# FFN down projection as 2x2 blocks with seven products, residual sum in DRAM

## The chip, the cores and the metric

The kernel runs on one core of one Trainium2 chip. The time is the device time of one launch in microseconds (us); the time before is the median of three runs. The profile is of one execution of the same program.

## What is computed

One layer of a hybrid encoder on 576 frames (512 of a new stream, 64 of a running one, the same weights for both): state-space heads and attention heads side by side, then an FFN, then a final norm. The change concerns the FFN alone; `x` there is what the two mixers and `w_out` have left.

```python
D_MODEL = 1024
D_FF = 2816          # 22 tiles of 128

def rmsnorm(x, w):
    return x * lax.rsqrt(jnp.mean(x * x, axis=-1, keepdims=True) + EPS) * w

x = x + jnp.concatenate([y_ssd, o], axis=-1) @ p['w_out']
hf = rmsnorm(x, p['norm_ffn'])
x = x + (jax.nn.silu(hf @ p['w_gate']) * (hf @ p['w_up'])) @ p['w_down']
y = rmsnorm(x, norm_final)
```

All in float32.

## The kernel before

**Layout.** Features lie on the 128 partitions and the T = 576 frames of both streams along the free axis, mostly in two halves of TH = 288 columns (`HC`). The residual `x2` is eight tiles of 128 x 576 in SBUF, one for each 128 of the 1024 features.

**Products.** A product of two float32 tiles is three matmuls: each operand is split into a high part (ScalarE's cast to fp32r, `wh_...`, L112) and a remainder (VectorE's subtraction, `wl_...`, L113), and high x high, high x low and low x high are summed in PSUM. `weights` (L119) loads 128 x 1024 raw weights on SyncE's queue and splits them.

**Gate and up.** For each of the FT = 22 FFN tiles f, `gu_steps` computes g (gate) and u (up) for both halves of the columns as one 2x2 block product with seven products in place of eight, m1 to m7, each with four contraction tiles (L852, 84 matmuls a tile). `gu_weights` makes the sums of weight blocks on VectorE (L809 to L812), `combine` and the steps m1 to m7 put the seven results together (copies of ScalarE at L914, L918, L922, additions of VectorE at L926 to L939; L935 and L939 are two of them). Three PSUM banks (tags sc, pp, hm) hold the results of a tile. The last two products of a tile, m4 and m3, are issued after m1 of the next one (`late`). `finish` takes silu of g (ScalarE), multiplies u by it (VectorE, L899) and splits the result into a high part and a remainder (`split_scaled`, L142 and L144): `prod[f]`, the operand of the down projection.

**Down.** CUTS divides the 22 tiles into five parts, of 5, 5, 4, 4 and 4. When the first tile of the next part has been computed, `down(fs)` runs the part just done: for each of the 8 output tiles t a weight tile of 128 x 128 for each f in it (`weights`, 512 or 640 columns, wr_d, wh_d, wl_d), and for each half of the columns `down_half` with 3 matmuls for each f (L953, ps_d), whose sum VectorE adds onto x2 (L966; in the first part x2 is first scaled by Ri, L965). The last part (f from LAST = 18 on) goes with the final norm: L953 ps_l with the weights wr_dl and the addition of `add` (L1005), then the outputs.

**Buffers.** tpool holds 7 tiles of one row of 576 (g, u and other temporaries), wpool 7 raw weight tiles, w2pool 11 split ones, cpool 5 pairs of rows (prod). midp's tags bc and sz hold x2. A tile that takes a buffer waits until the last reader of the one before is done.

**Order.** The steps are written as Python calls, but the order in which each engine issues its instructions is a list of numbers, ISSUE, one entry per engine, which is written into the program by hand or by a planner. Before, GpSimd has no instruction in the FFN's stage until the end.

## Time and profile before

| | before |
|---|---|
| median of 3 runs | 655.55 us (654.63 to 655.71) |
| span of the profiled execution | 651.7 us |
| median above the span | 3.9 us (655.55 - 651.7) |
| PE (TensorE) busy | 639.9 us, 98%, 4731 matmuls |
| DVE (VectorE) busy | 512.4 us, 79% |
| ACT (ScalarE) busy | 339.3 us, 52% |
| POOL (GpSimd) busy | 41.3 us, 6% |
| DMA | 63.22 MB, 97 GB/s over the span |

Busy times are sums over the span and say nothing of a single stage; the rows of the 40 slices, of stretches and of groups of instructions do. PE rows come one every 0.13 us where matmuls of 288 columns follow each other, though each row shows a duration of about 0.3 us, since they are pipelined. In the rows a name such as ps_d or wl_gu_S is the tile's name in the program without its numbers; "x165" is a count.

### The profile page before, as it was taken

The page shows a single profiled execution, that of the slowest core. Times are in us where ns is not written, and L with a number is a line of the kernel's source. Part 1 is how long each engine was busy: PE and PEld are TensorE (multiplying, and loading weights), DVE is VectorE, ACT ScalarE, POOL GpSimd, SP SyncE. Part 2 cuts the span into 40 slices and gives each one's busy share as a digit, 9 for nine tenths or more (in the row PEclk, how much of TensorE's full clock was granted, in tenths as well). Part 3 has the DMA queues.
Part 4 walks back from the last instruction along what each step waited for, and adds up shares of the span by engine and source line. Part 5 has one row for each costly group of instructions (what it writes and reads, how often), then busy time and mean ns, then how long its engine had stood idle before and what let it go on. Part 6 is the DMA issues. An engine that isn't in the chain of part 4 may idle for free.

```text
span 651.7 us, 11921 instructions
## 1 busy us (share of the span) xinstructions
PE 639.9 (98%) x4731; PEld 611.8 (94%) x4731; DVE 512.4 (79%) x935; ACT 339.3 (52%) x630; POOL 41.3 (6%) x80
## 2 busy tenths in 40 slices
PE   9999999998999999999999999999999999999995
PEld 8898989885787899999999999999999999999995
DVE  6899987899776699999996776775768577876655
ACT  7645426769674567665523445223533345334364
POOL 1321104001010000000000000000000000000023
PEclk9999999999999999999999999999999999999998
DMA  8312375323220232133422233311232224222004
GB/s 314 127 62 70 93 171 143 113 66 129 86 76 33 99 102 92 65 109 103 131 80 97 79 101 101 110 66 65 81 114 98 98 66 128 68 98 98 2 1 145
DMA packets 26151, 63.22 MB, mean 97 GB/s; under 512 B 3418, under 2 KB 10088, under 8 KB 25840
## 3 DMA queue, kind: packets, MB, share of 16 engines
q1 hardware_dynamic: 24560, 60.77, 28.3%
q0 software_dynamic: 816, 1.13, 0.8%
q8 instruction: 37, 0.61, 0.4%
q10 hardware_dynamic: 720, 0.57, 0.3%
q14 instruction: 18, 0.15, 0.1%
HBM read 58.03 MB, written 3.30 MB: 94 GB/s over the span
## 4 chain that ended last, share of the span: by engine, by line
PE 84%; DVE 3%; ACT 1%; DMA 1%; issue 1%; POOL 0%; POOLq 0%; DVEq 0%; ACTq 0%
PE ps_x L852 21%; PE ps_d L953 18%; PE ps_z L852 10%; PE ps_o L443 8%; PE ps_y L852 5%; PE ps_in L128 4%; PE ps_z L443 3%; PE ps_l L953 3%; PE ps_p L852 2%; PE sc L657 2%; PE pv L704 1%; PE ptp L679 1%; PE ps_v L590 1%; PE ps_q L443 1%; PE ps_y L527 1%
## 5 line engine op out<-in xcount | busy, mean ns | idle before, releaser
L953 PE MATMUL ps_d<-pr,wh_d 128*128 128x288 f32 x576 | 115.4, 294 | 0.0
L852 PE MATMUL ps_x<-xop,wh_gu_S 128*128 128x288 f32 x504 | 101.8, 295 | 0.0
L953 PEld LDWEIGHTS ps_d<-pr,wh_d 128*128 128x128 f32 x576 | 92.5, 188 | 0.0
L953 PE MATMUL ps_d<-pr,wl_d 128*128 128x288 f32 x288 | 84.6, 295 | 0.0
L852 PEld LDWEIGHTS ps_x<-xop,wh_gu_S 128*128 128x128 f32 x504 | 80.6, 188 | 0.2
L113 DVE TENSOR_TENSOR wl_gu_S<-gu,wh_gu_S 128x1024 fp32r<-128x1024 f32 x44 | 53.6, 1224 | 34.4 <-PE ps_y L852 13.8
L852 PE MATMUL ps_x<-xop,wl_gu_S 128*128 128x288 f32 x252 | 73.4, 295 | 0.0
L112 ACT CAST wh_gu_S<-gu 128x1024 fp32r<-128x1024 f32 x44 | 46.3, 1052 | 48.4 <-PE ps_d L953 25.4
L953 PEld LDWEIGHTS ps_d<-pr,wl_d 128*128 128x128 f32 x288 | 54.0, 188 | 0.0
L852 PEld LDWEIGHTS ps_x<-xop,wl_gu_S 128*128 128x128 f32 x252 | 47.0, 188 | 0.0
L128 PE MATMUL ps_in<-xs,wh_in 128*128 128x288 f32 x256 | 45.2, 298 | 1.2 <-DVE sp_a L351 1.0
L112 ACT CAST wh_d<-wr_d 128x640 fp32r<-128x640 f32 (+1 forms) x32 | 21.5, 673 | 39.1 <-PE ps_x L852 14.8
L128 PEld LDWEIGHTS ps_in<-xs,wh_in 128*128 128x128 f32 x256 | 37.5, 188 | 2.3 <-ACT up L381 1.2
L852 PE MATMUL ps_z<-xop,gu_a 128*128 128x288 f32 x252 | 38.0, 296 | 0.0
L852 PE MATMUL ps_z<-xop,wh_gu_S 128*128 128x288 f32 x168 | 36.0, 296 | 0.0
L852 PE MATMUL ps_x<-xop,wh_gu_A 128*128 128x288 f32 x168 | 35.3, 298 | 0.0
L852 PEld LDWEIGHTS ps_z<-xop,gu_a 128*128 128x128 f32 x252 | 35.1, 188 | 0.0
L852 PE MATMUL ps_y<-xop,wh_gu_A 128*128 128x288 f32 x168 | 34.2, 294 | 0.0
L966 DVE TENSOR_TENSOR x<-ps_d,x 128x288 f32<-128x288 f32 x64 | 28.8, 453 | 6.7 <-PE ps_d L953 6.5
L112 ACT CAST wh_gu_A<-gu 128x1024 fp32r<-128x1024 f32 x22 | 23.1, 1049 | 17.5 <-PE ps_d L953 11.5
L113 DVE TENSOR_TENSOR wl_gu_A<-gu,wh_gu_A 128x1024 fp32r<-128x1024 f32 x22 | 26.9, 1223 | 5.2 <-PE ps_x L852 3.9
L1049 POOL TENSOR_TENSOR fz<-fz,sq 128x320 f32<-128x320 f32 x3 | 2.6, 880 | 445.3 <-ACT sq L1044 445.3
(339 smaller groups left out, 1643.7 us busy)
## 6 DMA issues: line engine op xcount, KB each, us to landing
gu<-in_w_gu SPq DMA_DIRECT2D x44, 512.0 KB, 3.7
wr_d<-in_w_down SPq DMA_DIRECT2D x16, 320.0 KB, 2.9
wr_in<-in_w_in SPq DMA_DIRECT2D x8, 512.0 KB, 4.0
wr_out<-in_w_out SPq DMA_DIRECT2D x8, 512.0 KB, 3.2
wr_d<-in_w_down SPq DMA_DIRECT2D x16, 256.0 KB, 2.7
cumb<-cumD SPq DMA_DIRECT2D x5, 512.0 KB, 4.6
x<-in_xT SPq DMA_DIRECT2D x2, 1152.0 KB, 7.5
wr_z<-in_w_in SPq DMA_DIRECT2D x4, 512.0 KB, 4.4
```

The costliest lines, as they stand in the source:

```text
L112: act.copy(hi, raw)
L113: dve.tensor_tensor(lo, raw, hi.bitcast(F32), ALU.subtract)
L128: pe.matmul(ps[:m, hf, :n], w, x[:, hf * n : (hf + 1) * n], start=start and k == 0 and i == 0, stop=stop and k == last and i == 2,)
L443: pe.matmul(ps[:, :n], w, x[:, cols], start=k == 0 and i == 0, stop=k == len(terms) - 1 and i == 2,)
L527: pe.matmul(py[64 * j : 64 * j + 64, p * P : p * P + L], xdt[:L, h * HD : (h + 1) * HD], wts[:L, h, :L], start=True, stop=True,)
L590: pe.matmul(ps[:n], l, r, start=j == 0, stop=j == 2)
L657: pe.matmul(s[:, :nk], qs[:, j, q0 : q0 + P], ks[:, j, :nk], start=True, stop=True)
L679: pe.transpose(pp[:, k : k + P], prs[p, i][:, j, b * P : b * P + P], ident)
L704: pe.matmul(pv[64 * j : 64 * j + 64, b * P :], V[b][:, h * HD : (h + 1) * HD], pts[p, b, j], start=b == 0, stop=True, skip_group_check=b > 0,)
L852: pe.matmul(ps, p, q, start=not onto and first and kp == kps[0] and j == 0, stop=onto or (last and kp == kps[-1] and j == 2), skip_group_c ...
L953: pe.matmul(ps, w, x[:, cols], start=first and k == 0 and i == 0, stop=last and k == len(terms) - 1 and i == 2,)
L966: dve.tensor_tensor(x2[t][:, cols], ps, x2[t][:, cols], ALU.add)
```

## The change

The down projection of the 16 tiles f = 2 to 17 becomes 2x2 block products with seven products in place of eight. The tiles are taken as pairs (f even, f odd): the two feature tiles are the block rows of an operand, the two halves of the columns its block columns.

- `finish` hands a tile of PAIRED to `finish_pair`, which writes the product of u and g into the pair's tile (L915). After the second tile of a pair, `pair_operands` makes the combined operands (differences at L927 to L929: T1 to T4) and splits them into high parts (ScalarE, L936: 1152, 576 and 288 columns) and remainders (VectorE, L937). Two tiles with tags bc and sz, where x2 lay, hold part of them.
- `down_plain` takes the first part (f = 0 and 1) as before, but ScalarE copies its results out of PSUM and GpSimd writes them to `acc[1]` in DRAM; x2, scaled by Ri, is written to `acc[0]`.
- `down_steps(fs, m)` does a pair of output tiles (2m + 1 and 2m) for a part of four tiles: it loads the eight weight blocks in one transfer (wr_d), makes their eight sums on VectorE (ws_d, L1030 to L1034), splits both (L1038, L1039), and runs products m1, m6, m7, m2, m5, m4, m3 of six matmuls each in the manner of the gate/up steps (L1050). Products 6, 5 and 3 are added onto product 1 in one bank and 4 onto 7. ScalarE copies the seven intermediate results out of PSUM (L1061), and four transfers of GpSimd with addition (`send`, L1064) bring them into acc in DRAM: dd (288 columns), db, dc and da (576 columns each).
- Two of the four steps of a part stand after the first tile of the next part, two after the second.
- After the last step the residual comes back into two tiles `sum`: a plain load of acc[0] for four tiles each on SyncE's queue (L1143) and additions of acc[1] by GpSimd, two tiles each (L1145).
- CUTS is (0, 2, 6, 10, 14, 18, 22), and the order of every engine from the FFN's stage on is a new one.

The core of the diff (empty lines left out):

```diff
     def finish(f, g, u):
         act.activation(g, g, AF.Silu)
+        if f in PAIRED:
+            finish_pair(f, g, u)
+            return
         dve.tensor_tensor(u, u, g, ALU.mult)
         s = slot(cpool, "c", f"pr{f}")
         split_scaled(s, u, None)
         prod[f] = hilo(s)
+    raw_pair, pair_ops, pair_tiles, pending = {}, {}, [], []
+    def finish_pair(f, g, u):
+        k, second = f // 2, f % 2
+        if not second:
+            raw_pair[k] = slot(cpool, "c", f"up{k}")
+        b = raw_pair[k]
+        dve.tensor_tensor(b[:, second], u, g, ALU.mult)
+        if second:
+            pending.append(lambda: pair_operands(k))
+    def pair_operands(k):
+        b = raw_pair[k]
+        if len(pair_tiles) < 2:
+            pair_tiles.append(midp.tile([P, 4, T], F32, tag=("bc", "sz")[len(pair_tiles)], name=f"pair{k}"))
+        z = pair_tiles[(k - 1) % 2].rearrange("p a b -> p (a b)").bitcast(F32R)
+        b = b.rearrange("p a (h n) -> p (a h) n", h=2)
+        d13, d4 = tmp(f"d13_{k}").rearrange("p (a n) -> p a n", a=2), tmp(f"d4_{k}", TH).unsqueeze(1)
+        dve.tensor_tensor(d13, b[:, 0:2], b[:, 1:4:2], ALU.subtract)
+        dve.tensor_tensor(b[:, 1], d13[:, 1], b[:, 0], ALU.subtract)
+        dve.tensor_tensor(d4[:, 0], b[:, 1], b[:, 2], ALU.add)
+        bh, bl = (slot(cpool, "c", f"{n}{k}").bitcast(F32R).rearrange("p a (h n) -> p (a h) n", h=2) for n in ("uph", "upl"))
+        th, tl = (z[:, 3 * TH * i : 3 * TH * i + 3 * TH].rearrange("p (a n) -> p a n", a=3) for i in range(2))
+        ops = {}
+        for raw, hi, lo, names in (
+            (b, bh, bl, ("B11", "T2", "B21", "B22")), (d13, th[:, 0:2], tl[:, 0:2], ("T1", "T3")), (d4, th[:, 2:], tl[:, 2:], ("T4",)),
+        ):
+            act.copy(hi, raw)
+            dve.tensor_tensor(lo, raw, hi.bitcast(F32), ALU.subtract)
+            for i, n in enumerate(names):
+                ops[n] = hi[:, i], lo[:, i]
+        pair_ops[k] = ops
...
-    def down_terms(fs, t):
-        w = weights(a["w_down"][t][:, fs[0] * P : (fs[-1] + 1) * P], len(fs) * P, f"d{fs[0]}_{t}")
-        return [(wk(w, k), prod[f]) for k, f in enumerate(fs)]
+    acc = [dpool.tile([KT, P, T], F32, name=f"acc{i}") for i in range(2)]
...
-    def down(fs):
-        for t in range(KT):
-            terms = down_terms(fs, t)
+    def down_plain(fs, ts):
+        n = 1024 // (len(fs) * P)
+        for t in ts:
+            if t % n == 0:
+                raw = wslot(wpool, f"wr_d{t}")
+                sp.dma_start(
+                    raw.rearrange("p (t c) -> p t c", t=n),
+                    a["w_down"][t : t + n][:, :, fs[0] * P : (fs[-1] + 1) * P].rearrange("t p c -> p t c"),
+                )
+                w = split_weights(raw, f"d{t}")
+            terms = [(wk(w, t % n * len(fs) + k), prod[f]) for k, f in enumerate(fs)]
+            dn = tmp(f"dn{t}")
             for hf, cols in enumerate(HC):
-                ps = fbank(("hm", "sc", "pp")[(2 * t + hf) % 3], f"ps_d{fs[0]}_{t}")
+                ps = fbank(("hm", "sc", "pp")[(2 * t + hf) % 3], f"ps_d{t}")
                 down_half(ps, terms, cols)
-                if fs[0] == 0:
-                    dve.tensor_tensor(x2[t][:, cols], x2[t][:, cols], Ri[:, cols], ALU.mult)
-                dve.tensor_tensor(x2[t][:, cols], ps, x2[t][:, cols], ALU.add)
-    CUTS = (0, 5, 10, 14, LAST, FT)
+                act.copy(dn[:, cols], ps)
+            pool.dma_start(acc[1][t], dn)
+            dve.tensor_tensor(x2[t], x2[t], Ri, ALU.mult)
+            pool.dma_start(acc[0][t], x2[t])
+    DOWN = {
+        1: (0, 4, "B11"), 2: (0, 5, "B21"), 3: (1, 6, "B22"), 4: (0, 1, "T4"), 5: (1, 0, "T1"), 6: (1, 4, "T2"), 7: (1, 2, "T3"),
+    }
+    def down_steps(fs, m):
+        ks = [f // 2 for f in fs[::2]]
+        blocks = lambda z: z.rearrange("p (c n) -> p c n", n=P)
+        raw, sums = wslot(wpool, f"wr_d{fs[0]}_{m}"), wslot(wpool, f"ws_d{fs[0]}_{m}")
+        r, q = blocks(raw), blocks(sums)
+        sp.dma_start(
+            raw.rearrange("p (t c) -> p t c", t=2),
+            a["w_down"][2 * m : 2 * m + 2][:, :, fs[0] * P : (fs[-1] + 1) * P].rearrange("t p c -> p t c"),
+        )
+        four = lambda z: z.rearrange("p (a b) n -> p a b n", a=2)
+        dve.tensor_tensor(
+            four(q[:, 0:4]), r[:, 0:4:2].unsqueeze(1).to_broadcast([P, 2, 2, P]), four(r[:, 1:7])[:, :, 0:3:2], ALU.add,
+        )
+        dve.tensor_tensor(q[:, 4:6], q[:, 0:2], r[:, 4:8:2], ALU.add)
+        dve.tensor_tensor(q[:, 6:8], q[:, 4:6], r[:, 5:8:2], ALU.add)
+        w = []
+        for z, b0 in ((r, 1), (q, 0)):
+            hi, lo = (blocks(wslot(w2pool, f"d{fs[0]}_{m}_{len(w)}{i}", F32R)) for i in "hl")
+            act.copy(hi[:, b0:], z[:, b0:])
+            dve.tensor_tensor(lo[:, b0:], z[:, b0:], hi.bitcast(F32)[:, b0:], ALU.subtract)
+            w.append((hi, lo))
+        x, y, z = (fbank(tag, f"ps_d{fs[0]}_{m}") for tag in ("sc", "pp", "hm"))
+        def product_of(i, ps, onto=False):
+            src, b0, name = DOWN[i]
+            hi, lo = w[src]
+            for n, k in enumerate(ks):
+                b = b0 + (n if src else 2 * n)
+                xhi, xlo = pair_ops[k][name]
+                for j, (p, v) in enumerate(((hi[:, b], xhi), (hi[:, b], xlo), (lo[:, b], xhi))):
+                    pe.matmul(
+                        ps, p, v, start=not onto and n == 0 and j == 0, stop=onto or (n == len(ks) - 1 and j == 2),
+                        skip_group_check=onto,
+                    )
+        db, dd = (stage[i][m % 2] for i in range(2))
+        da, dc = (tmp(f"{z}{fs[0]}_{m}") for z in ("da", "dc"))
+        L, R = HC
+        t0, t1 = 2 * m + 1, 2 * m
+        def put(out, ps, sign=1.0):
+            (act.copy(out, ps) if sign > 0 else act.mul(out, ps, sign))
+        def send(i, out, src):
+            pool.dma_start(out, src, accum_op=ALU.add)
+        def m1():
+            product_of(1, x)
+            put(dd, x)
+            send(0, acc[0][t0][:, L], dd)
+        def m6():
+            product_of(6, x, True)
+            put(db[:, L], x, -1.0)
+        def m7():
+            product_of(7, z)
+            put(dc[:, R], z)
+        def m2():
+            product_of(2, y)
+            put(da[:, L], y)
+        def m5():
+            product_of(5, x, True)
+            put(db[:, R], x, -1.0)
+            send(0, acc[0][t1], db)
+        def m4():
+            product_of(4, z, True)
+            put(dc[:, L], z)
+            send(1, acc[1][t1], dc)
+        def m3():
+            product_of(3, x, True)
+            put(da[:, R], x)
+            send(1, acc[1][t0], da)
+        return m1, (m4, m3), (m6, m7, m2, m5)
+    CUTS = (0, 2, 6, 10, 14, LAST, FT)
+    PAIRED = range(2, LAST)
     PARTS = tuple(range(i, j) for i, j in zip(CUTS, CUTS[1:]))
+    stage = []
     gu_first()
     late = ()
     for part in PARTS:
         for f in part:
             if f:
                 first, rest, middle = gu_steps(f)
-                for step in (first, *late, *middle):
+                for step in (first, *late):
+                    step()
+                while pending:
+                    pending.pop()()
+                for step in middle:
                     step()
                 late = rest
-            if f == part[0] and f:
+            half = f - part[0]
+            if f < 2 or half > 1:
+                continue
+            if prev[0] in PAIRED:
+                if not stage:
+                    stage.extend(((fz[:, 0], fz[:, 2]), (fz[:, 3, :TH], fz[:, 3, TH:])))
+                for m in (2 * half, 2 * half + 1):
+                    first, rest, middle = down_steps(prev, m)
+                    for step in (first, *late, *middle):
+                        step()
+                    late = rest
+            else:
                 for step in late:
                     step()
                 late = ()
-                down(prev)
+                down_plain(prev, range(4 * half, 4 * half + 4))
         prev = part
     for step in late:
         step()
     tc.keep_in_program_order(act.preload_act_table_set("natural_log_exp_and_others"))
+    x2.clear()
+    for i2, tag in enumerate(("bc", "sz")):
+        x2t[i2] = z = midp.tile([P, 4, T], F32, tag=tag, name=f"sum_{i2}")
+        rows = lambda i, n: acc[i][n].rearrange("t p c -> p t c")
+        sp.dma_start(z, rows(0, slice(4 * i2, 4 * i2 + 4)))
+        for j in (0, 2):
+            pool.dma_start(z[:, j : j + 2], rows(1, slice(4 * i2 + j, 4 * i2 + j + 2)), accum_op=ALU.add)
+        x2.extend(z[:, j] for j in range(4))
...
     "POOL": """
-0-3 7 18 28 4 8 5 9 6 10 26 11 27 12 29 13-17 20-23 19 24-25 31 30 32-42 53 55 57 59 54 56 58 60 43-52 61-73
+0-3 7 18 28 4 8 5 9 6 10 26 11 27 12 29 13-17 20-23 19 24-25 31 30 32-42 53 55 57 59 54 56 58 60 43-52 61-69 71 73 75
+70 77 79 81 74 76 72 83 78 80 82 84-87 89 88 90 92 91 93-103 105 104 106 108 107 109-119 121 120 122 124 123 125-135
+137 136 138 140 139 141-143 145 144 146-148
...
```

**VectorE at the start of a down projection.** Before, in the stretch where the fourth part is brought down (x is the residual, wl_d a weight's remainder, gu a sum of gate/up weights, u and g the next tile's results):

```order
L935 TENSOR_TENSOR u_6400<-ps_z_6403,u_6400 128x288
L966 TENSOR_TENSOR x_0_2048<-ps_d_0_6538,x_0_2048 128x288
L811 TENSOR_TENSOR gu_2_6806<-gu_2_6806,gu_0_6804 128x512
L113 TENSOR_TENSOR wl_d_4_6671<-wr_d_4_6668,wh_d_4_6670 128x512
L966 TENSOR_TENSOR x_0_2048<-ps_d_0_6552,x_0_2048 128x288
L810 TENSOR_TENSOR gu_3_6807<-gu_1_6805,gu_0_6804 128x512
L812 TENSOR_TENSOR gu_3_6807<-gu_0_6804,gu_2_6806 128x512
L113 TENSOR_TENSOR wl_d_5_6705<-wr_d_5_6702,wh_d_5_6704 128x512
```

The additions onto x, each on a matmul's result, alternate with weight rows.

Now, at the start of the second part of pairs, f = 6 to 9 (up is the pair's tile, d_4 the differences, pair and upl the remainders, ws_d the sums of weight blocks, d_0_1l and d_1_0l weight remainders):

```order
L1030 TENSOR_TENSOR ws_d_1_5139<-wr_d_1_5138 128x512
L1039 TENSOR_TENSOR d_0_1l<-ws_d_0_5054,d_0_1h 128x1024
L915 TENSOR_TENSOR up_4861<-u_4817,g_4816 128x576
L927 TENSOR_TENSOR d_4_4987<-up_4861 128x576
L928 TENSOR_TENSOR up_4861<-d_4_4987,up_4861 128x288
L929 TENSOR_TENSOR d_4_4988<-up_4861 128x288
L937 TENSOR_TENSOR pair_4174<-d_4_4987,pair_4174 128x576
L1033 TENSOR_TENSOR ws_d_1_5139<-ws_d_1_5139,wr_d_1_5138 128x256
L1034 TENSOR_TENSOR ws_d_1_5139<-ws_d_1_5139,wr_d_1_5138 128x256
L937 TENSOR_TENSOR upl_4993<-up_4861,uph_4992 128x1152
L969 TENSOR_TENSOR u_4942<-ps_x_4943,u_4942 128x288
L1039 TENSOR_TENSOR d_1_0l<-wr_d_1_5138,d_1_0h 128x896
```

No row of VectorE reads ps_d any more; the pair's operands (L927 to L937) stand between weight rows, and the remainder of 1152 columns is the sixth row after the product of u and g.

**ScalarE in the first step (m = 0) of that part.** Before, ScalarE has casts of wr_d here and no row that reads ps_d. Now (fz is the staging tile for db and dd, the ACTIVATE rows are copies with a factor of -1, wh_gu are gate/up weights):

```order
L1061 COPY fz<-ps_d_0_5067 128x288
L814 CAST gu_a_5220<-gu_1_5211 128x512
L112 CAST wh_gu_A_5222<-gu_0_5210 128x1024
L1061 ACTIVATE fz<-ps_d_0_5067 128x288
L1061 COPY dc_0_5071<-ps_d_0_5069 128x288
L1061 COPY da_0_5070<-ps_d_0_5068 128x288
L1061 ACTIVATE fz<-ps_d_0_5067 128x288
L1061 COPY fz<-ps_d_1_5152 128x288
L112 CAST wh_gu_S_5226<-gu_2_5212 128x1024
L1061 COPY da_0_5070<-ps_d_0_5067 128x288
```

The copies of one bank stand between casts of the next gate/up tile's weights.

**SyncE at the end.** Before, the four weight tiles of the last part are followed by the outputs:

```order
L119 DMA wr_dl_7186<-in_w_dlast 128x1024
L119 DMA wr_dl_7192<-in_w_dlast 128x1024
L119 DMA wr_dl_7198<-in_w_dlast 128x1024
L119 DMA wr_dl_7204<-in_w_dlast 128x1024
L1025 DMA out_yT<-x_0_2048 128x2x320
```

Now the loads of the residual stand around the fourth:

```order
L119 DMA wr_dl_7386<-in_w_dlast 128x1024
L119 DMA wr_dl_7392<-in_w_dlast 128x1024
L119 DMA wr_dl_7398<-in_w_dlast 128x1024
L1143 DMA sum_7378<-acc_3185 128x4x576
L119 DMA wr_dl_7404<-in_w_dlast 128x1024
L1143 DMA sum_7382<-acc_3185 128x4x576
L1183 DMA out_yT<-sum_7378 128x2x320
```

The load of the first half of the residual stands ahead of the fourth weight tile, that of the second half behind it.

More of the change, by code (lines that the diff above doesn't have):

```diff
@@ L1187 @@
 419 464 425 422 424 415 433 431 426 432 429 428 427 438 430 434 469 463 436 435 437 439 442 441 443 466 440 444 451
[L1188 to L1191 removed]
+465 446 467-468 452-453 445 447 455 454 448 473 475 456 477 476 474 457 472 470 478 458-459 449-450 479 460 481 480
+461 471 482 491 487 483 496-497 484 488 498-499 489 500-502 485-486 503 510 490 515-518 522 492 504 519 506 520 507
+521 508 532-535 539 546 493-495 536 547-549 505 511-512 509 523 537 529-530 524-525 513-514 531 538 540 528 550 541
+566 526 542 527 551 543 545 552 544 567-568 553-554 569 555 574 570 556-559 561 575-576 560 565 577 562 578-581 571
+582-583 572 563 590-591 584 592 585-586 564 598 573 599-600 593-594 587-588 601 589 603 602 595 604-607 596 610 597
+608-609 620-623 611 627 612 624 613-614 625-626 619 634-636 628 637 617 638 618 629 616 615 630 641 639 631 640 633
+632 654-656 642 657 643 662 658 644-647 649 663-664 648 653 665 650 666-669 659 670-671 660 651 678-679 672 680
+673-674 652 686 661 687-688 681-682 675-676 689 677 691 690 683 692-695 684 698 685 696-697 708-711 699 715 700 712
+701-702 713-714 707 722-724 716 725 705 726 706 717 704 703 718 729 727 719 728 721 720 742-744 730 745 731 750 746
+732-735 737 751-752 736 741 753 738 754-757 747 758-759 748 739 766-767 760 768 761-762 740 774 749 775-776 769-770
+763-764 777 765 779 778 771 780-783 772 786 773 784-785 796-799 787 803 788 800 789-790 801-802 795 810-812 804 813
+793 814 794 805 792 791 806 817 815 807 816 809 808 830-832 818 833 819 839 834 820-823 825 840-841 824 829 842 826
+843-846 835 847-848 836 827 855-856 849 857 850-851 828 864 837 865-866 858 838 859 852-853 867 854 869 868 860
+870-873 861 876 862 874 880 875 881-883 887 884 863 885 877 886 879 878 888-898
 """,
@@ L1211 @@
 11-14 16 15 17-20 23 22 25 21 24 31 26 32 39-40 36 33 38 41-42 37 43-47 55 77 62 79 54 56 58 63 81 57 60 59 61 68 66
[L1212 removed]
+72 67 65 76 69-71 78 73 86 64 74-75 87 80 88-89 84 90 85 91 98 101 99-100 102-103 106-165
 """,
```

28 lines of the change are left out of this document (17 added, 11 removed).

## The prediction

> **What bounds the kernel now.** I read the page first: busy times, the 40 slices, the chain that ended last.
>
> ```profile
> PE 639.9 (98%) x4731; PEld 611.8 (94%) x4731; DVE 512.4 (79%) x935; ACT 339.3 (52%) x630; POOL 41.3 (6%) x80
> PEclk9999999999999999999999999999999999999998
> PE 84%; DVE 3%; ACT 1%; DMA 1%; issue 1%; POOL 0%; POOLq 0%; DVEq 0%; ACTq 0%
> PE ps_x L852 21%; PE ps_d L953 18%; PE ps_z L852 10%; PE ps_o L443 8%; PE ps_y L852 5%; PE ps_in L128 4%; PE ps_z L443 3%; PE ps_l L953 3%; PE ps_p L852 2%; PE sc L657 2%; PE pv L704 1%; PE ptp L679 1%; PE ps_v L590 1%; PE ps_q L443 1%; PE ps_y L527 1%
> ```
>
> TensorE is 98% busy at a granted clock of 0.9 or more in nearly every slice, and the chain runs through its matmuls; the down projection (L953, ps_d) is 18% of the span. What a removed matmul is worth I read from the stretches and from the chain in order of time.
>
> ```profile
> core 0: us, PE busy (x) PEld busy (x) DVE busy (x) ACT busy (x) POOL busy (x), PEclk, DMA share, GB/s
> 250.00:300.00 50.00, 50.00 (x371) 49.19 (x371) 49.48 (x87) 32.30 (x53) 0.00 (x0) 1.00 0.25 84
> 430.00:500.00 70.00, 70.00 (x530) 70.00 (x529) 50.16 (x82) 29.56 (x45) 0.00 (x0) 1.00 0.27 88
> 490.20 21.87 PE ps_d L953 x165
> 560.29 21.87 PE ps_d L953 x165
> ```
>
> From the start of one down projection's run of 165 matmuls to the next one's lie 70.09 us. In it stand four gate/up steps of 84 matmuls and one down projection of 192, 528 in all: 0.1327 us for each. The stretch 430 to 500 holds about one such period with no gap on TensorE, and VectorE works 50 of its 70 us. So here a matmul taken out is worth 0.1327 us, as long as nothing else comes to wait.
>
> **What is removed.** The 18 tiles before LAST cost 18 x 8 x 2 x 3 = 864 matmuls; now 2 x 48 = 96 in down_plain and 16 steps of 7 products x 2 pairs x 3 = 672, together 768. The products are as wide (288 columns) and the lists of the two programs differ by 96 on TensorE. **Gain at most 96 x 0.1327 = 12.7 us**, 3.2 us in each of the four sets of four tiles: a period of 70.1 becomes 66.9 us. That is the whole gain; all else must hide under it.
>
> **VectorE.** I price it by the distance between starts, since rows overlap a little.
>
> ```profile
> 286.65 0.69 DVE L809 TENSOR_TENSOR gu<-gu 128x512 f32<-128x512 f32 x1
> 287.25 0.46 DVE L935 TENSOR_TENSOR u<-ps_z,u 128x288 f32<-128x288 f32 x1
> 287.62 0.69 DVE L811 TENSOR_TENSOR gu<-gu,gu 128x512 f32<-128x512 f32 x1
> 288.21 2.36 DVE L113 TENSOR_TENSOR wl_gu_S<-gu,wh_gu_S 128x1024 fp32r<-128x1024 f32 x2
> 290.49 0.46 DVE L939 TENSOR_TENSOR g<-ps_x,R 128x288 f32<-128x288 f32 x1
> 290.85 0.76 DVE L899 TENSOR_TENSOR u<-u,g 128x576 f32<-128x576 f32 x1
> 291.52 0.69 DVE L820 TENSOR_TENSOR gu_a<-gu,gu_a 128x512 fp32r<-128x512 f32 x1
> L113 DVE TENSOR_TENSOR wl_d<-wr_d,wh_d 128x640 fp32r<-128x640 f32 (+1 forms) x32 | 24.1, 756 | 5.7 <-issue 1.9 <-PE ps_d L953 1.5 <-ACT g L898 1.4
> L966 DVE TENSOR_TENSOR x<-ps_d,x 128x288 f32<-128x288 f32 x64 | 28.8, 453 | 6.7 <-PE ps_d L953 6.5
> ```
>
> Back to back, 512 columns take 0.60 us, 288 take 0.37, 576 take 0.67 and 1024 take 1.14 (2.28 for two); by the line through these I put 256 at 0.33, 896 at 1.00 and 1152 at 1.27. A period of four tiles then costs VectorE:
> - four gate/up steps of four sums and a remainder at 512, three remainders at 1024, five combinations at 288 (8.3 us) and one product of u and g (0.67): 35.9 us, against 4 x 9.6 before, since the second 576 row (L144) goes for paired tiles;
> - two pair_operands of 0.67 + 0.37 + 0.37 + 1.27 + 0.67 + 0.37 = 3.7 us: 7.4 us, new;
> - four down steps of sums 0.60 + 0.33 + 0.33 and remainders 1.00 + 1.14 = 3.4 us: 13.6 us, in place of eight remainders (L113 wl_d) and sixteen additions (L966), about 10.7 us.
>
> Sum 57 of 66.9 us, 85%, where the same sum for before gives 49 of 70.1 and the stretch 430 to 500 measured 50.16. VectorE stays under TensorE. The stretch 250 to 300 shows that it can run full (49.48 of 50 us) while TensorE has no gap, so 85% alone costs nothing. What can cost is order: after the last product of a pair's second tile come the product of u and g, the differences, ScalarE's 1152-wide copy and VectorE's 1152-wide remainder, until the first product of the next set needs them. From the end of that last product to the use lie four products and a few matmuls, some 8 us; the chain's own work (0.37, 0.69, 0.67, 0.67, 0.37, about 1.2 on ScalarE, 1.27) is 5.2, and about 2.8 us of other VectorE rows stand between. It comes out even to within half a microsecond. I put **0.4 us a set, 1.5 us in all**, bounds 0 and 3 a set.
>
> **ScalarE** takes over the evacuation: seven copies per down step, and casts of 896 and 1024 columns.
>
> ```profile
> L112 ACT CAST wh_gu_S<-gu 128x1024 fp32r<-128x1024 f32 x44 | 46.3, 1052 | 48.4 <-PE ps_d L953 25.4
> L918 ACT COPY u<-ps_x 128x288 f32<-128x288 f32 x17 | 6.8, 397 | 16.3 <-PE ps_x L852 16.3
> 400.23 0.30 PE L852 MATMUL ps_x<-xop,wl_gu_S 128*128 128x288 f32 x1
> 400.62 0.40 ACT L918 COPY u<-ps_x 128x288 f32<-128x288 f32 x1 [2.53 <-PE ps_x L852]
> ```
>
> A step costs it 7 x 0.40 + 0.93 + 1.05 = 4.8 us, in place of two casts wh_d and nothing else; the set rises from 29.6 (in 70 us) to about 46 of 66.9. Product 6 adds onto product 1 in the same bank, product 5 onto 6 and 3 onto 5, so each waits for a copy. A copy ends 0.1 + 0.4 us after the matmul's row, 0.8 after the matmul's slot; between two products onto one bank stand two others, 12 x 0.1327 = 1.6 us. That leaves 0.8 us for a cast of 1.05 in front of the copy: the cover is thin, and where a cast starts last, up to 0.3 us shows. That is within the 0.4 us a set.
>
> **GpSimd's transfers** are what before does not have: 64 that add to DRAM, four per step (144 KB and three of 288 KB, 1.03 MB), 4.1 MB a set.
>
> ```profile
> 39.35 0.59 POOL L311 DMA_DIRECT2D out_ckvT<-ckf  x1 [0.33 <-DVE ckf L310]
> 97.34 3.83 POOL L601 DMA_DIRECT2D qs<-rrp  x8 [10.31 <-DVE rrp L423]
> 99.20 1.22 DVE L113 TENSOR_TENSOR wl_z<-wr_z,wh_z 128x1024 fp32r<-128x1024 f32 x1
> out_ckvT<-ckf POOLq DMA_DIRECT2D x1, 288.0 KB, 2.5
> x<-in_xT SPq DMA_DIRECT2D x2, 1152.0 KB, 7.5
> q1 hardware_dynamic: 24560, 60.77, 28.3%
> ```
>
> Issue: 0.59 us each for 128 rows, 2.4 us a step against 5.6 us of matmuls; GpSimd has nothing else there, so no one queues behind. The eight issues at 97 us took 0.48 us each beside VectorE's TENSOR_TENSOR rows. The Trainium skill's page "SBUF — State Buffer" (sections "SBUF: two separate sides" and "Who interferes with whom") warns that VectorE in a two-port mode locks GpSimd out of writing descriptors, about 3.1 us in place of 0.62 for a transfer; it excepts tensor_tensor. By the warning alone the 64 issues would cost 200 us of queue; by the row, and VectorE runs only TENSOR_TENSOR in this stage, 38 us.
>
> Landing: no row adds to memory. Ends: 2.5 us, the plain 288 KB write of this queue, and 7.5, the 1152 KB load. I take 5.0, twice the nearest row, since an addition has to read what it adds to as well. The page "Collectives: The Full Stack" (section "Why ReduceScatter is half of AllGather") has the same factor: adding costs no cycles of its own, the second read halves the rate. No run here shows it yet.
> Who waits: stage and tmp buffers come free when the addition lands. The tightest is the buffer of product 4 of a set's third step, which the next tile's u takes. By the program's order 66 matmuls (8.8 us) pass from that product's end to the copy that writes u, and 24 more (3.2) until TensorE needs it: 12.0, less 2.0 to 2.5 for two copies and a cast, leaves 9.5 us. At 5.0 nothing shows, at 7.5 neither.
> Rate: q1 moved 60.77 MB in 28.3% of 651.7 us, 330 GB/s when busy; half of that is 165, and weights take 27% of the engines, which leaves 120 GB/s. A set's 4.1 MB leave within some 36 us, 115 GB/s, and have 66.9 us until they repeat, 62. It fits.
>
> **The end.** The residual sum comes back: two loads of 1152 KB and four additions of 576 KB, once the pair tiles are free.
>
> ```profile
> 618.51 15.46 PE ps_l L953 x112
> 625.74 2.88 DVE L1005 TENSOR_TENSOR x<-ps_l,x 128x320 f32<-128x320 f32 x7 [3.71 <-PE ps_l L953]
> ```
>
> The tiles come free at product 4 of the last step. From there to the last gate/up product are 177 matmuls, 23.5 us, and from 618.51 to the first addition of ps_l 7.2 more: 30.7 us. The load takes 7.5, the additions twice 7.5 for each half: 22.5 us. On SyncE the fourth wr_dl stands behind the first load's wait and is needed 20 us later. Price 0, with 8 us of cover. If the additions take twice as long again, 37.5 us: 7 us late. The 16 plain writes of 288 KB in f = 2 and 3 are issued by GpSimd while TensorE does 12 matmuls a tile; VectorE has fewer rows there than before. Price 0.
>
> **Sum.** -12.7 + 1.5 = -11.2 us. The profiled execution's span is 651.7 us; the runs' median of 655.55 (654.63 to 655.71) lies 3.9 above it, what is outside the span, which the change leaves alone. So span 640.5 and median 644.4. About 0.2% is what a measurement of this kernel can tell from no change, 1.3 us.
>
> **The rivals.**
> 1. *Engines in each other's way*: the even chain above and the thin cover of the copies miss by 1 to 2.5 us a set and not 0.4. For it: VectorE from 72 to 85%, ScalarE from 42 to 69%. Against: the full stretch at 250. Time 655.55 - 12.7 + 4 x 1.75 = 650.
> 2. *Slower: the adding transfers bound the set.* If they move at well under half the plain rate, the queue does not drain before the next set, u's buffer comes late, ScalarE stands at that copy, and TensorE behind it. It decides at 4.1 MB in 70.1 us, 59 GB/s, which with the weights' 27% means 81 GB/s, a quarter of 330. At 73 GB/s a set takes 77 us: 655.55 + 4 x 7.1 = 684. For it: 1.13 MB of GpSimd's queue are all that before shows, none adds. Against: four times slower than plain is far from the factor that the second read gives.
> 3. *The sum comes back late*: 7 us, 651, from 30.7 us on.
>
> That the matmuls do not go is excluded: the order on TensorE holds 96 fewer.
>
> **How the numbers follow.** Forecast (642 to 647.5) 0.57; rival 1 0.11; rival 3 0.04: faster 0.72. Rival 1 at its bound of 3 us a set eats 12 of the 12.7 us: same 0.03. Slower 0.25: rival 2 with 0.20, a VectorE that falls behind by more than 3.2 us a set 0.05. The range reaches from 642 (12.7 and a little at the ends) to 662, which takes in the forecast, rivals 1 and 3, no change and the mildest of the slower cases: 0.8.
>
> **What would show it.** Right: a period of 66.9 to 67.5 us between the first matmuls of two sets; VectorE 55 to 60 us busy in it; landings of the L1064 transfers near 5 us; the first ps_l addition not waiting for a transfer. Wrong: waits of u's or g's copy (L956, L952) for a transfer of GpSimd, landings above 9.5 us (rival 2); idle TensorE before ps_d or ps_x with a copy or a remainder as releaser (rival 1); the addition L1163 behind the sum tiles (rival 3).

## The result, and the profile after

The changed kernel takes 644.18 us (643.54 to 644.58, four runs) where the kernel before takes 655.63: a ratio of 0.983 [0.982, 0.985], the 95% interval in brackets. Run again on another occasion it took 643.84 against 654.3, 0.984 [0.982, 0.986]. It is faster by 10.5 to 11.5 us. The forecast was 644.4; the sum behind it was 11.2.

The page of the changed kernel, busy times and the chain that ended last:

```profile
PE 626.6 (98%) x4635; PEld 598.8 (93%) x4635; DVE 543.0 (85%) x945; ACT 400.7 (62%) x768; POOL 110.2 (17%) x164
PE 83%; DVE 3%; ACT 1%; issue 1%; DMA 1%; POOL 1%; POOLq 0%; DVEq 0%; ACTq 0%
```

4635 matmuls in place of 4731, and TensorE is as full as it was; the chain is still its own. The chain in order of time has two unbroken runs of 66 matmuls of the down projection in each part of four tiles; the first of them is shown for three parts (start, length). Below them a stretch of 67 us shows what lies beside it (TensorE, weight loads, VectorE, ScalarE, GpSimd, granted clock, DMA share, GB/s):

```profile
414.69 8.77 PE ps_d L1050 x66
481.57 8.77 PE ps_d L1050 x66
548.46 8.77 PE ps_d L1050 x66
434.00:501.00 67.00, 67.00 (x507) 67.00 (x506) 59.26 (x89) 43.14 (x75) 13.90 (x16) 1.00 0.70 158
```

From part to part lie 66.88 and 66.89 us, where the forecast had 66.9 and, with stalls, up to 67.5. In that stretch TensorE has no gap; VectorE works 59.3 us (forecast 57, 55 to 60), ScalarE 43.1 (forecast 46), GpSimd 13.9, and the DMA engines are busy for 0.70 of it.

**Where the time went.** The FFN, from its first ps_p matmul to the end of the long run of ps_l matmuls below, lasts 379.35 us before (254.62 to 633.97) and 366.57 after (255.26 to 621.83): 12.78 us, 96 x 0.133. The end gives some of it back. The run of ps_l, before and after, and the DRAINs with which GpSimd's queue closes the program (their number; shortest, middle and longest in ns; first and last start):

```profile
618.51 15.46 PE ps_l L953 x112
L1301 POOLq DRAIN  x3: 46/102/3489, 646.6 to 651.5; - x3
```

```profile
606.52 15.31 PE ps_l L988 x111
L1482 POOLq DRAIN  x3: 46/93/7051, 634.4 to 642.0; - x3
```

From the end of ps_l to the first DRAIN pass 12.6 us in both. But this first one of the three DRAINs, the long one (the expectations call it the last DRAIN), lasts 7.05 us in place of 3.49, and from the end of ps_l to the end of the span pass 20.4 us in place of 17.8. That is 2.63 us and not 3.56: in the kernel before another 0.96 us pass between the end of this DRAIN and GpSimd's next row, in the changed one only 0.05. The spans differ by 9.5 us (651.7 and 642.2): 12.78 less 2.63, less the 0.64 by which the FFN begins later in this execution. (In experiments 1 to 3 and 6, which share everything ahead of the FFN, it begins at 254.3 to 255.5, so the 0.64 is not the change's.) The medians differ by more, since the profiled execution of before was a short one: on the later occasion its runs lie 1.7 to 2.0 us above their own spans, not 3.9.

### The profile page after: what moved, and what is told of

It reads as the page before. It is cut to its first block, busy times and chain, and to the rows that moved or that the text cites. A ratio compares the mean times of both kernels' runs of the same rounds, so it can differ in the third digit from the quotient of the medians.

```text
span 642.2 us, 12089 instructions
## 1 busy us (share of the span) xinstructions
PE 626.6 (98%) x4635; PEld 598.8 (93%) x4635; DVE 543.0 (85%) x945; ACT 400.7 (62%) x768; POOL 110.2 (17%) x164
## 4 chain that ended last, share of the span: by engine, by line
PE 83%; DVE 3%; ACT 1%; issue 1%; DMA 1%; POOL 1%; POOLq 0%; DVEq 0%; ACTq 0%
PE ps_x L852 21%; PE ps_d L1050 14%; PE ps_z L852 10%; PE ps_o L443 8%; PE ps_y L852 5%; PE ps_in L128 4%; PE ps_z L443 3%; PE ps_l L988 3%; PE ps_d L988 2%; PE ps_p L852 2%; PE sc L657 2%; PE pv L704 1%; PE ptp L679 1%; PE ps_v L590 1%; PE ps_q L443 1%
## 5 line engine op out<-in xcount | busy, mean ns | idle before, releaser
L113 DVE TENSOR_TENSOR wl_gu_S<-gu,wh_gu_S 128x1024 fp32r<-128x1024 f32 x44 | 53.5, 1221 | 10.5 <-ACT wh_gu_S L112 6.9
L1064 POOL DMA_DIRECT2D acc<-fz x32 | 28.0, 910 | 167.3 <-ACT fz L1061 138.5
L443 PE MATMUL ps_o<-cat_y,wh_out 128*128 128x288 f32 x128 | 29.3, 312 | 0.4 <-ACT cat_y L142 0.4
L852 PEld LDWEIGHTS ps_z<-xop,wh_gu_S 128*128 128x128 f32 x168 | 27.2, 189 | 0.3 <-ACT wh_gu_S L112 0.3
L128 PE MATMUL ps_in<-xs,wl_in 128*128 128x288 f32 x128 | 27.4, 296 | 0.0
L852 PEld LDWEIGHTS ps_x<-xop,wh_gu_A 128*128 128x128 f32 x168 | 27.1, 189 | 0.1
L852 PEld LDWEIGHTS ps_y<-xop,wh_gu_A 128*128 128x128 f32 x168 | 26.9, 188 | 0.0
L443 PE MATMUL ps_z<-xs,wh_z 128*128 128x288 f32 x128 | 26.4, 299 | 0.0
```

Of the source, the lines that this page charges most:

```text
L113: dve.tensor_tensor(lo, raw, hi.bitcast(F32), ALU.subtract)
L128: pe.matmul(ps[:m, hf, :n], w, x[:, hf * n : (hf + 1) * n], start=start and k == 0 and i == 0, stop=stop and k == last and i == 2,)
L443: pe.matmul(ps[:, :n], w, x[:, cols], start=k == 0 and i == 0, stop=k == len(terms) - 1 and i == 2,)
L852: pe.matmul(ps, p, q, start=not onto and first and kp == kps[0] and j == 0, stop=onto or (last and kp == kps[-1] and j == 2), skip_group_c ...
L1064: pool.dma_start(out, src, accum_op=ALU.add)
```

## The experiments

Where an experiment issues more instructions than the changed kernel, a helper `more(nc, f)` places those that f makes right behind the last one of their engine (or ahead of a given one), so that the planned order of all others stays.

### 1. Eight products

```diff
-            product_of(2, y)
+            product_of(2, y); more(nc, lambda: product_of(2, y))
```

> The changed kernel with product 2 of every down step computed twice into the same bank: 96 matmuls more, everything else and every order the same. Theory (TensorE's matmuls set the end, all else is hidden): 644.2 + 96 x 0.133 = 657.0 us, a period of 66.9 + 3.2 = 70.1 us, no gap on TensorE. Rival a (part of the gain is relief of VectorE, or the new order): it stays below the kernel before, 652 us or less. Rival b (there is idle time in the sets that the added matmuls fill): 655 us.

Measured: 657.64 us against 654.3, 1.006 [1.004, 1.008]; the FFN takes 379.71 us, 0.36 more than before. TensorE has no gap, the 66.88 us become 70.2:

```profile
417.45 10.39 PE ps_d L1050 x78
487.63 10.39 PE ps_d L1050 x78
```

With 96 matmuls put back the whole gain is gone, and 3.3 us more (2.4 to 5.0 by the interval): the seven products' matmuls are all that the change wins. The residual in DRAM, the relief of VectorE from additions and the new order together win nothing here; what is lost beside the 0.36 us is the longer end.

### 2. Writes in place of additions

```diff
-            pool.dma_start(out, src, accum_op=ALU.add)
+            pool.dma_start(out, src)
```

> The changed kernel with the 64 transfers of the down steps as plain writes, without the addition (so the residual sum is left out). Theory (they are hidden): 644.2 us within 1; the landings fall from 6 to 8 us to about 4, the DMA share of a set from 0.69 to about 0.48, as an addition moves its bytes twice. Rival (the additions hold something up): faster than 643 us, and waits of u's copy for a transfer, 2.0 us now, that were worth something. If an addition cost no more than a write, landings and share would stay.

Measured: 647.31 us, 0.989 of before [0.988, 0.991], so 3 us slower than with additions. The DMA issues (KB each, median us to landing), after and here, and the same stretch as above:

```profile
acc<-fz POOLq DMA_DIRECT2D x16, 288.0 KB, 6.3
acc<-dc POOLq DMA_DIRECT2D x16, 288.0 KB, 8.2
```

```profile
acc<-fz POOLq DMA_DIRECT2D x16, 288.0 KB, 4.5
acc<-dc POOLq DMA_DIRECT2D x16, 288.0 KB, 3.6
434.00:501.00 67.00, 67.00 (x507) 67.00 (x506) 59.29 (x90) 43.21 (x75) 8.63 (x16) 1.00 0.49 157
L1482 POOLq DRAIN  x3: 46/98/10355, 634.7 to 645.5; - x3
```

The FFN takes 366.58 us, the same to 0.01: the additions are hidden. Of the DMA engines' time they take twice what writes take: with 0.27 for weights (the share of the stretch 430 to 500 before) 0.43 in place of 0.22. Their landings are longer by a factor of 1.4 to 2.3: 8.2 and not 3.6 us for dc, 7.8 and not 3.5 for da, 6.3 and not 4.5 for db (fz). The 3 us are all GpSimd's long DRAIN at the end, 10.36 us. No theory had that.

### 3. TensorE in the order of the calls

Four places in TensorE's row of numbers, of which the first reads:

```diff
-2105-2221 2234-2236 2240-2241 2222-2233 2237 2242-2248 2238-2239 2249-2725
+2105-2221 2222-2725
```

> The changed kernel with TensorE's order put back to the order of the calls at the start of the four paired parts: the seven or so gate/up matmuls that stand between the halves of the first product 1 go behind it; 5 to 8 matmuls move at each place, none is added. Theory (the even chain of the prediction, hidden by the order): the matmul that reads upl comes at about 478.0 in place of 479.0 in the third part and upl is written until 478.7: 0.7 us idle before ps_d in each part, 647 us in all. Rival (the chain has slack of its own): 644.2, no idle time there.

Measured: 647.59 us, 0.990 [0.988, 0.991]; the FFN takes 370.06 us, 3.5 more, and a part 67.74 to 67.78 in place of 66.88. The chain at the start of a part, and what TensorE waits for in the FFN (us in total, times, longest):

```profile
406.51 0.68 DVE up L915
407.21 0.77 DVE d L927
408.00 0.47 DVE up L928
408.50 0.46 DVE d L929
408.96 0.67 DVE pair L937
409.63 0.35 DVE ws_d L1033
410.00 0.42 DVE ws_d L1034
410.43 1.28 DVE upl L937
411.75 0.53 PE ps_d L1050 x2
PE ps_d L1050 <- DVE upl L937: 1.4, 4, 0.3
```

These are VectorE's rows from the product of u and g (L915) on, one behind the other: the prediction's product, differences and remainder, with the other rows of VectorE that it put between them (six rows stand between L915 and the remainder of 1152 columns). ScalarE's cast of uph, which the prediction had on the chain, is not on it: it ends at 410.03, before VectorE comes to upl. They do end last as soon as the order does not make room for them: the matmul on upl comes 0.64 us after the one before it and the next another 0.23 later, where 0.13 is the step, so 0.6 us are lost. The other 0.26 us of a part are lost at 409.03, where a gate/up product onto ps_x starts 0.05 us after the end of ScalarE's copy of ps_x (L956, 408.58 to 408.98); the profile names no releaser for so short a gap. In the changed kernel's own order the same place reads:

```profile
477.31 1.35 DVE L937 TENSOR_TENSOR upl<-up,uph 128x1152 fp32r<-128x1152 f32 x1
477.97 0.29 PE L1050 MATMUL ps_d<-uph,d_0h 128*128 128x288 f32 x1
478.10 1.09 PE L852 MATMUL ps_z<-xop,gu_a 128*128 128x288 f32 x7
479.03 0.30 PE L1050 MATMUL ps_d<-upl,d_0h 128*128 128x288 f32 x1
```

Seven gate/up matmuls stand between the matmul that needs uph and the one that needs upl; upl ends at 478.66 and is used at 479.03. The three matmuls on the part's first pair stand ahead of that product onto ps_x there, at 475.86, so that TensorE has work until the copy is done.

### 4. No planned order in the FFN

```diff
-        order = list(_places(text))
+        order = [n for n in _places(text) if n < MADE[engines[name].engine]]
```

MADE holds how many instructions each engine has ahead of the FFN.

> The changed kernel without the planned order from the first gate/up tile on: the framework's own list of instructions stands there. Theory (the seven products need the order, since each step's chains have a microsecond or less of cover): slower than 650 us, with idle TensorE before ps_x and ps_d, perhaps slower than before. Rival (the removed matmuls alone carry the gain, whatever the order): within 2 us of 644.2.

Measured: 681.27 us, 1.041 [1.038, 1.044]. The span is 36 us longer than the changed kernel's, and TensorE waits for operands in each part; the two largest of its waits (us in total, times, longest):

```profile
PE ps_d L1050 <- DVE pair L937: 5.3, 3, 1.9
PE ps_x L852 <- DVE u L969: 3.2, 1, 3.2
```

Smaller waits and many short gaps make up the rest. The same instructions are 27 us slower than the kernel before. The order does not make the gain, but without one it is lost and 27 us more. (The kernel before was not run without its own.)

### 5. The plain writes on ScalarE's queue

```diff
-            pool.dma_start(acc[1][t], dn)
+            MORE.update({n: (tuple(halves_of[-2:]), 1) for n in more(nc, lambda: act.dma_start(acc[1][t], dn))}); GONE.append(next_pool(nc))
...
-            pool.dma_start(acc[0][t], x2[t])
+            GONE.append(next_pool(nc)); later.append(lambda t=t: act.dma_start(acc[0][t], x2[t]))
```

MORE and GONE adapt the lists of numbers. Each write to acc[1] stands behind ScalarE's two copies of its tile; the eight writes to acc[0] are issued in two groups of four (`later`), the first of them behind the last copies (L1012 x4 below).

> The changed kernel with the 16 plain writes to DRAM (L1009, L1012) issued by ScalarE in place of GpSimd; nothing else moves. What it is for: GpSimd's last DRAIN lasts 3.49 us before, 7.05 in the changed kernel and 10.36 with plain writes in place of the 64 additions, and the span ends with it. Theory a (it grows with the transfers that GpSimd has issued, 24 before and 108 now, 42 ns each): 6.4 us, 0.7 us faster than the changed kernel. Theory b (plain writes alone make it longer): 3.5 us, 3 us faster, 641. Theory c (only the last transfers, the reload, count): 7.05 us and no change. The 16 issues on ScalarE hold nothing up in any of them.

Measured: 649.71 us, 0.994 [0.992, 0.996], 6 us slower than the changed kernel. The long DRAIN is 1.0 us shorter, between theories a and b, but the issues are not free on an engine that works in order (ScalarE's rows and its wait):

```profile
316.31 3.24 ACTq L1012 DMA_DIRECT2D acc<-x  x4
319.64 0.40 ACT L952 COPY g<-ps_x 128x288 f32<-128x288 f32 x1 [3.73 <-DVE x L1011]
PE ps_x L852 <- ACT g L952: 4.2, 2, 3.1
L1520 POOLq DRAIN  x3: 46/93/6064, 640.9 to 647.4; - x3
```

The copy of g stands behind four issues, those wait for VectorE's L1011, and TensorE waits for g: 4.2 of the 6 us, while the rest lies in some twenty gaps of about 0.1 us. All three theories had put the issues at nothing.

### 6. The changed kernel again

> The changed kernel itself beside the others on the same chip: the first comparison gave 0.983 of before, 644.2 us. Every theory expects the same ratio here, 0.982 to 0.985.

Measured: 643.84 us, 0.984 [0.982, 0.986]; the long DRAIN is 7.05 us again.

### 7. Each addition twice, to the same rows

```diff
-            pool.dma_start(out, src, accum_op=ALU.add)
+            pool.dma_start(out, src, accum_op=ALU.add); more(nc, lambda: pool.dma_start(out, src, accum_op=ALU.add))
```

> The changed kernel with each of the 64 adding transfers sent twice in a row (so the sum holds each part twice): 8.2 MB a set in place of 4.1. Theory (they are hidden now; a set's 4.1 MB take 0.42 of the DMA engines' time and the weights 0.27): 0.42 x 2 + 0.27 = 1.11, so the transfers bound a set at 1.11 x 66.9 = 74 us, 7 us over, 672 us in all or some more, with waits of u's and g's copies for the transfers. Rival (the limit on landing, 9.5 us, is passed long before the rate): over 690 us. Rival (the DMA share overstates them): under 650 us. GpSimd's last DRAIN, if it goes by the count of transfers: 9.7 us.

Measured: 870.47 us, 1.330 [1.327, 1.333]. All theories missed, since the experiment tests something else: the second addition to the same rows waits on GpSimd until the first has landed.

```profile
POOL acc L1064 <- DMA acc<-fz: 147.3, 30, 7.4
POOL acc L1064 <- DMA acc<-dc: 76.3, 14, 7.7
POOL acc L1064 <- DMA acc<-da: 72.2, 14, 6.6
```

58 waits of some 5 us, 296 us on a queue that works in order. They are waits for a semaphore, so the program itself holds the second addition back; they say nothing of the rate. In the changed kernel no two transfers to the same rows follow each other closely: a row of acc comes up again a set later.

### 8. Each transfer twice, to rows of their own

```diff
-            pool.dma_start(out, src, accum_op=ALU.add)
+            pool.dma_start(out, src, accum_op=ALU.add); more(nc, lambda: pool.dma_start(out2, src, accum_op=ALU.add))
```

out2 are the same rows of two tiles `aside`; the 16 plain writes are doubled in the same way (not shown).

> The changed kernel with each transfer of the down steps and of f = 2 and 3 sent a second time, to rows of DRAM that nobody reads, so that no transfer has to wait for its twin: 8.3 MB a set. Theory (a set's own 4.1 MB take 0.42 of the DMA engines' time, weights 0.27): 1.11 of 66.9 us, a set of 74 us or more, 672 us or more; waits of u's and g's copies for transfers. Rival (the engines can take more than this share shows): 644 to 650. Against the run with the same rows twice (870 us) it tells the rate from the wait for a landing.

Measured: 681.17 us, 1.041 [1.037, 1.045]. The same stretch, a landing, ScalarE's waits, and one of VectorE at the end:

```profile
434.00:501.00 67.00, 60.12 (x432) 59.66 (x431) 49.63 (x74) 35.72 (x60) 21.48 (x25) 0.95 0.86 195
acc<-dc POOLq DMA_DIRECT2D x16, 288.0 KB, 12.2
ACT u L956 <- DMA aside<-dc: 18.8, 3, 6.5
ACT g L952 <- DMA aside<-dc: 15.1, 4, 3.9
DVE sum L1163 <- DMA sum<-acc: 5.3, 2, 3.4
```

432 matmuls in 67 us and not 507, and a set takes 75.5 to 76.9 us where the rate alone would give 74 or more. The wait stands where rival 2 had put it, u's copy (L956) behind dc: landings of 12 to 13 us are above the limit of 9.5. The DMA engines are busy for 0.86 of this stretch and not for all of it, so these rows don't tell a full set of engines from transfers that come in bunches. Rival 2 is a real mechanism, which begins between 4.1 and 8.3 MB a set. Rival 3 shows here as well: the last row is the addition of ps_l (L1163) waiting for the reload, and behind it TensorE waits 7.3 us, a fifth of the 37 us.

### 9. More work for ScalarE ahead of a copy

```diff
-            put(db[:, L], x, -1.0)
+            c = put(db[:, L], x, -1.0); more(nc, lambda: [act.copy(pair_tiles[1][:, 3].bitcast(F32R), R2) for _ in range(3)], c)
```

> The changed kernel with three casts of 576 columns, 1.74 us together, ahead of ScalarE's copy of product 6 in each of the 16 down steps; they write columns that nobody reads. Theory (the prediction's thin cover of 0.8 us between that copy and product 5, and ScalarE waits some 0.3 us for product 6): 0.6 us late in each step, 10 us in all, 654 us, idle TensorE before ps_d with that copy as releaser. Rival (the copies have more slack than that, since ScalarE is idle a third of the time): within 2 us of 644.

Measured: 666.61 us, 1.018 [1.017, 1.020]; the FFN ends 22.8 us later, 1.42 a step.

```profile
501.02 2.08 ACT L1073 CAST pair<-R 128x576 fp32r<-128x576 f32 x3
503.01 0.40 ACT L1061 ACTIVATE fz<-ps_d 128x288 f32<-128x288 f32 x1
PE ps_d L1050 <- ACT fz L1061: 18.3, 16, 1.4
```

The casts take 1.98 us from start to start, not 1.74, and 0.56 of it is covered, on average over the 16 steps. The cover is as thin as the prediction said, and thinner than its 0.8: ScalarE idles for a third of the time and has little more than half a microsecond to spare at this place.

### 10. and 11. More work for VectorE

```diff
-            w.append((hi, lo))
+            w.append((hi, lo)); more(nc, lambda: [dve.tensor_tensor(pair_tiles[0][:, 3].bitcast(F32R), R2, R2, ALU.add) for _ in range(1)])
```

(and `range(2)`; the line runs twice in a step, once for each half of the weights)

> The changed kernel with two additions of 576 columns (0.67 us each) more on VectorE behind the remainders of each of the 16 down steps; they write columns that nobody reads. 5.4 us a set: VectorE's rows go from 59.3 to some 64.6 of 66.9 us. Theory (a VectorE under TensorE's time costs nothing but order): 0 to 1 us a set, 644 to 648 us. Rival (the order is so tight that every microsecond more of VectorE shows): 5.4 us a set, 666.

> The same with four additions in each step: 10.7 us a set, 68 to 70 us of VectorE in a set of 66.9 of TensorE. Theory: VectorE becomes the bound, a set takes 68 to 70 us and the whole 649 to 657 us, with TensorE idle before ps_x and ps_d and rows of VectorE as releasers (or copies that wait for them). Rival (VectorE's rows overlap, so it is really far from full): within 2 us of the run with two.

Measured: 650.72 us, 0.994 [0.993, 0.996], and 676.59, 1.033 [1.032, 1.035]. The same stretch with two and with four, and under the second two waits of its whole FFN:

```profile
434.00:501.00 67.00, 66.32 (x496) 65.72 (x495) 62.56 (x96) 42.46 (x73) 13.28 (x16) 1.00 0.66 152
```

```profile
434.00:501.00 67.00, 62.03 (x461) 61.06 (x461) 62.34 (x94) 38.48 (x67) 12.12 (x14) 1.00 0.63 146
PE ps_x L852 <- ACT u L956: 10.4, 5, 2.7
ACT u L956 <- DMA acc<-dc: 5.0, 3, 2.7
```

Over the changed kernel's 643.84 that is 6.9 and 32.8 us: 5.4 us more cost 1.7 a set, 10.7 cost 8.2. So 2.5 to 3.7 us are covered, and of the step from two to four all shows. VectorE is never full: with four it works 62 of 67 us, and TensorE waits. That this is its order alone is not shown. ScalarE's copies wait for VectorE, but TensorE's largest wait is for u's copy (L956), which in turn waits 5.0 us for the landing of dc: the place of rival 2, reached with the transfers of the changed kernel. Against both expectations the first lies between theory and rival, the second above its theory.

### 12. A later reload

```diff
-            pool.dma_start(z[:, j : j + 2], rows(1, slice(4 * i2 + j, 4 * i2 + j + 2)), accum_op=ALU.add)
+            pool.dma_start(z[:, j : j + 2], rows(1, slice(4 * i2 + j, 4 * i2 + j + 2)), accum_op=ALU.add); (i2, j) == (1, 0) and more(nc, lambda: pool.dma_start(...))
```

> The changed kernel with one of the four additions of the reload (that for t = 4 and 5) sent twice in a row; the second waits for the first to land and the one for t = 6 and 7 stands behind it (so t = 4 and 5 hold that part twice). Theory (the last pair is issued at 600 and lands by 610, the first addition of ps_l is at 613.7, so some 4 us of cover are left): a landing of 8.7 us more makes it 4 to 5 us late, 648.5 us, with L1163 waiting for a transfer. By the prediction's 8 us of cover: 645. Rival (the end has slack behind L1163): 644.2.

Measured: 643.71 us, 0.985 [0.982, 0.987], as the changed kernel. GpSimd's and VectorE's rows:

```profile
599.67 2.44 POOL L1145 DMA_DIRECT2D sum<-acc  x2 [1.67 <-DVE g L964]
608.29 1.20 POOL L1145 DMA_DIRECT2D sum<-acc  x1 [6.17 <-DMA sum<-acc]
613.39 2.88 DVE L1163 TENSOR_TENSOR sum<-ps_l,sum 128x320 f32<-128x320 f32 x7 [3.71 <-PE ps_l L988]
```

The repeated addition went out last of all, at 608.29: the one for t = 6 and 7 did not stand behind it, as the expectation had it, but went ahead (the second of the two at 599.67). Still L1163 waits for TensorE and not for it. In the trace it lands at 614.47, and the fifth row of L1163, the first that needs it, starts at 614.99. So an addition for t = 4 and 5 that is issued 8 us later costs nothing, with 0.5 us to spare. My 4 us of cover were reckoned to the first row of L1163, which needs t = 0 alone.

## Why the prediction was right

**The gain.** 96 x 0.1327 = 12.7 us was forecast, 12.78 measured in the FFN; eight products take it away.

**VectorE and the even chain.** The prices by the line between sizes hold for rows that follow each other freely (1152 columns from 477.31 to the next start 1.27 us). They are too low where a row reads the result of the one just before it: 0.79 us from L927 to L928 in experiment 3 (407.21 to 408.00), where 0.67 was taken. The sum for a set was 57 us, the stretch has 59.3. The chain was forecast even to within half a microsecond and priced at 0.4 us a part; it costs 0 in the planned order and 0.6 without the moved matmuls, 0.9 with the copy beside it (experiment 3). The step that failed is the size of this term, 1.5 us in all. The cover was counted rightly: from the end of the last product to the use of upl lie 60 matmuls, 8.0 us (471.07 to 479.03), the seven held back among them. The chain takes 7.6 of them, so 0.37 us are left over and nothing shows.

**ScalarE's copies.** Forecast within that term; no stall is seen in the changed kernel. The cover is 0.56 and not 0.8 us (experiment 9).

**The transfers.** The factor two of an addition over a write in the DMA engines' time is shown (experiment 2). The Trainium skill's page "Collectives: The Full Stack" (section "Why ReduceScatter is half of AllGather") has it for the reducing step of a collective; these runs agree, 0.43 against 0.22. The landing was put at 5.0 and is 6.3 to 8.2 us for 288 KB, near the limit of 9.5; u's copy does wait for a transfer now and then (what L956 waited for: us, times), mostly for da and not for product 4's dc, and none of it reaches TensorE. An issue on GpSimd, forecast at 0.59 us, lasts 0.91 for an addition (0.54 for a plain write in experiment 2):

```profile
  DMA acc<-da: 2.0, 2
L1064 POOL DMA_DIRECT2D acc<-fz x32 | 28.0, 910 | 167.3 <-ACT fz L1061 138.5
```

So the place of rival 2 was right, u's copy, and its room smaller than I had it. The rate is 144 GB/s (4.13 MB in 0.43 of 66.9 us) where 165 was taken, if all that the share grew by is the additions'. The lockout of GpSimd that the Trainium skill's page "SBUF — State Buffer" (section "Who interferes with whom") warns of does not show beside VectorE's TENSOR_TENSOR rows, as its exception has it: the longest of the 64 issues takes 1.2 us.

**The end.** The reload takes 29.1 us (from the first load's issue at 581.5 to the last landing at 610.6) and not the 22.5 of the forecast: its second load waits for the last additions of the steps, which I had not counted (SyncE's wait), and the loads land in 10.7 us and not 7.5.

```profile
SPq L1143 <- DMA acc<-fz: 6.3, 1, 6.3
sum<-acc SPq DMA_DIRECT2D x2, 1152.0 KB, 10.7
```

It is hidden all the same (experiment 12). What I had nowhere is GpSimd's long DRAIN, 2.63 us of the span.

**The span and the median.** "3.9 us outside the span, which the change leaves alone" was wrong: about 2 of it was that the profiled execution was a short one. By the span the forecast was 640.5 and 642.2 was measured. That the median was met to 0.2 us is luck: the stalls that did not come (1.5 us) and the smaller distance from the span (1.7 and not 3.9) stand against the DRAIN (2.63) and the later beginning of the FFN (0.64). The mechanism, 96 matmuls at 0.133 us with all else hidden, was right without luck.

## What to carry to other kernels

Where one engine is full without gaps, price a change by that engine's instructions alone, and then look at each cover by its place in the order and not by an engine's share: in this kernel ScalarE at two thirds had 0.56 us to spare at one copy, VectorE at 88% some 3 us in a set. Read the order of the full engine too: whoever planned it may have put other work just where a chain ends late. And count what a queue leaves behind at the end of the program.

## What the runs showed of the hardware

In these runs an addition to DRAM took the DMA engines' time of two writes: a share of 0.43 and not 0.22 for the same bytes, with landings of 6.3 to 8.2 and not 3.5 to 4.5 us. GpSimd's long DRAIN at the end lasted 3.49 us after 24 transfers issued by GpSimd, 6.06 after 92, 7.05 after 108, 7.14 after 109 (experiment 12), but 10.36 after 108 with plain writes in place of additions, 6.20 after 188 (experiment 8) and 5.17 after 172 (experiment 7). It is the same to 0.01 us in kernels with the same transfers at other times, so it goes by what was issued, but not by the count alone; what sets it stays open.
